# Query blocks loaded two ahead, projection weights rounded at set row blocks, scan outputs begun later

## The chip, the core and the metric

The kernel runs on one core of a Trainium2 chip. The time is the device time of one execution in microseconds (us); lower is better. TensorE (PE) multiplies matrices, VectorE (DVE), ScalarE (ACT) and GpSimd (POOL) do elementwise work, and SyncE (SP) issues nearly all transfers (DMA) of this kernel. Operands lie in SBUF, sums of products in the banks of PSUM.

## The reference

One decoder layer, float32, one sequence of 1024 tokens of width 1024. A normalised input is projected for two groups of heads that work side by side; their outputs are joined, projected and added to the input, and a squared-ReLU MLP follows. Cut to what matters:

```python
h = rms_norm(x, norm1_w)
proj = h @ w_in
da_q, da_k, da_v, dn_qkv, dn_z, dn_a, dn_b = jnp.split(proj, [...], axis=-1)
# group A: 4 heads, two 64-wide softmax maps each, causal, 128-wide values
da_q, da_k = rms_norm(da_q, q_norm_w), rms_norm(da_k, k_norm_w)
da_o = (softmax(q1 k1^T) - lam * softmax(q2 k2^T)) @ v       # per head
da_o = rms_norm(da_o, da_out_norm_w) * (1 - lam_init)
# group B: 4 heads, causal convolution, then the gated delta rule, a scan over chunks
dn_o = gated_delta_rule(dn_q, dn_k, dn_v, g, beta)
dn_o = rms_norm(dn_o, dn_out_norm_w) * silu(dn_z)
x = x + concatenate([da_o, dn_o]) @ w_out
h = rms_norm(x, norm2_w)
x = x + square(relu(h @ w_up)) @ w_down
```

## The kernel before

Products of weights and activations are made in three passes: each operand is split into a rounded part (`hH`, `wH`, type float32r) and the remainder (`hL`, `wL`), and `wH*hH + wL*hH + wH*hL` is accumulated in PSUM. A weight is therefore loaded raw (`wraw`), copied with rounding by ACT (L199) and subtracted by DVE (L200).

Up to about 239 us the gates and the projections of group B run. Then several streams are interleaved on PE by hand. Class `Interleave` (L39) holds Python generators with priorities and a planned time `now`; each `yield` says from when, or from which PSUM bank on, a stream may go on, `flow.pe` advances the time by a piece of PE work, `flow.chain` books time on the planned queues of ACT ("S"), DVE ("V") and POOL ("G") and returns when a chain of operations would be done, and `flow.hold` keeps a bank until then. The result is a fixed order of PE's instructions (L1456). The order on the other engines, SP with its transfers among them, is chosen by the framework's scheduler, which simulates a timeline; on each engine instructions then run in that order, and each waits for its operands. `tc.issue_after(ins)` keeps an instruction behind another one on the same engine.

The streams that matter here:

- `scan` (L801) and `scan_out` (L855): the delta rule over eight chunks of 128 tokens. For each chunk, `scan_out` loads two blocks per head (`pkb`, five buffers) and the gate (`zgt`), waits until 2500 ns after its start by the plan, makes two groups of products in bank `pB`, normalises and stores them. After the last chunk it sets `state["scan"]`, which lets other streams start.
- `da_units` (L940): the projections of group A in six units, (keys, queries, values) for each of two pairs of heads. A unit has 256 columns of weights in four quarters and goes over eight row blocks `tb` of 128 tokens, 24 matmuls each (L962 to L964). At block 0 of a unit, `load_unit` (L185) is called for the next unit (after the last unit, for a half of the output weights): four loads on SP's queue into two raw buffers, four roundings. Four weight buffers (`wH0`, `wH1`, `wL0`, `wL1`) alternate. `unit_time` books ACT and DVE for it and gives the planned time of each quarter. A block ends with a copy out of PSUM into `qn` (four buffers, L973 or L981); keys and queries are normalised, transposed in `da_turns` (L919) and stored to DRAM; values are stored as they are.
- `scores` (L1032): for each of 32 pairs of a head and a row block, queries are fetched by `load_q` (L1019) into `qa` and `qb` (two buffers each, four transfers), scores are made for two maps (L1082 to L1085), DVE takes the maximum (L1087), ACT the exponential (L1091). The load for the next pair is written right behind a pair's work.
- `values` (L1107): transposes the weights of a pair (L1123), copies them (L1125), multiplies by the values (L1135) into a bank of `px`, copies the result out (L1144), squares the copy for the norm (L1145) and scales it (L1149).
- `mixed` and `outproj` (L1182, L1212): transposes of the joined rows and the output projection, which fill PE beside the later attention.

From about 650 us on, the two products of the MLP run in a form with seven products in place of eight.

Of the kernel before, what the change touches and what calls it, by code (L numbers as in the profile page):

```python
# [9 lines left out]
F32 = mybir.dt.float32  # L10
# [8 lines left out]
P = 128  # L19
# [101 lines left out]
def tile_hymba_layer(  # L121
# [60 lines left out]
    hH = hpool.tile([P, KB, SEQ], F32R, name="hH")  # L182
    hL = hpool.tile([P, KB, SEQ], F32R, name="hL")

    def load_unit(src, ranges, k0=0, nk=KB, eng=None, rp=None):  # L185
        eng = eng or V
        width = sum(n for _, n in ranges)
        wh, wl = staged("wH"), staged("wL")
        wh = wh[:, :nk * width].rearrange("p (k c) -> p k c", k=nk)
        wl = wl[:, :nk * width].rearrange("p (k c) -> p k c", k=nk)  # L190
        st = 2 * UC // width
        for k in range(0, nk, st):
            raw = rp.tile([P, 2 * UC], F32, tag="wraw", name="wraw", bufs=8) if rp else laid("wraw")
            raw = raw[:, :st * width].rearrange("p (k c) -> p k c", k=st)
            o = 0
            for c0, n in ranges:
                nc.sync.dma_start(raw[:, :, o:o + n], src[:, k0 + k:k0 + k + st, c0:c0 + n])
                o += n
            S.copy(wh[:, k:k + st, :], raw)  # L199
            eng.tensor_tensor(wl[:, k:k + st, :], raw, wh[:, k:k + st, :].bitcast(F32), ALU.subtract)  # L200
        return wh, wl

    def mm3(ps, lh, ll, rh, rl, n):
# [651 lines left out]
    def scan_out(c, Sold, yy):  # L855
        pkb = {}
        for h in range(HEADS):
            pkb[h] = sb.tile([P, 2, P], F32, tag="pkb", name="pkb", bufs=5)
            nc.sync.dma_start(pkb[h], park_d[h, c, :, 3:5, :])
        zgt = sb.tile([P, 512], F32, tag="zgt", name="zgt", bufs=1)  # L860
        nc.sync.dma_start(zgt, zg_d[c])
        oc = sb.tile([P, 512], F32, tag="oc", name="oc", bufs=2)
        so = sb.tile([P, 4], F32, tag="so", name="so", bufs=2)
        osq = sb.tile([P, P], F32, tag="osq", name="osq", bufs=1)
        yield flow.now + 2500, "pB"
        if c > 0:
            o1 = pB.tile([P, 512], F32, tag="pB", name="ps_o1")
            for h in range(HEADS):
                T.matmul(o1[:, h * P:(h + 1) * P], pkb[h][:, 0, :], Sold[h], start=True, stop=True)
            V.tensor_tensor(v4(oc), v4(o1), bc_col(eg[:, c::8]), ALU.mult)  # L870
            flow.pe(4 * MM)
            flow.hold("pB", flow.chain(vec(512)))
            yield flow.now, "pB"
        o2 = pB.tile([P, 512], F32, tag="pB", name="ps_o2")
        for h in range(HEADS):
            T.matmul(o2[:, h * P:(h + 1) * P], pkb[h][:, 1, :], yy[h], start=True, stop=True)
        if c > 0:
            V.tensor_tensor(oc, oc, o2, ALU.add)
        else:
            S.copy(oc, o2)  # L880
        for h in range(HEADS):
            i = cidx(h, c)
            S.activation(osq, oc[:, h * P:(h + 1) * P], AF.Square, scale=rq[:, i:i + 1], accum_out=so[:, h:h + 1])
        f = sb.tile([P, 4], F32, tag="of", name="of", bufs=2)
        rstd(f, so, 1.0 / P, EPS, sb, "oft", 4)
        V.tensor_tensor(f, f, rq[:, c::8], ALU.mult)
        for h in range(HEADS):
            V.scalar_tensor_tensor(oc[:, h * P:(h + 1) * P], oc[:, h * P:(h + 1) * P], f[:, h:h + 1],
                                   zgt[:, h * P:(h + 1) * P], ALU.mult, ALU.mult)
        nc.sync.dma_start(mixn_d[c], oc)  # L890
        flow.pe(4 * MM)
        t = flow.chain(vec(512))
        flow.hold("pB", t)
        flow.chain(*[act(P, True)] * 4, vec(4), powr(4), vec(4), *[vec(P, 60)] * 4, start=t)
        if c == NT - 1:
            s2ctx.close()
            spctx.close()
            mp = ctx.enter_context(tc.tile_pool(name="mp", bufs=1, **left))
            pools["mp"] = mp
            for tb in tiles:  # L900
                accs[tb] = row_tile("acc")
            pools["a2"] = bctx.enter_context(tc.tile_pool(name="a2", bufs=1, **left))
            pools["be"] = bctx.enter_context(tc.tile_pool(name="be", bufs=2, **left))
            pools["rsc"] = scctx.enter_context(tc.tile_pool(name="rsc", bufs=1, space=PSUM, **right))
            state["scan"] = True
# [34 lines left out]
    def da_units():  # L940
        todo = [(g, kind) for g in range(2) for kind in (1, 0, 2)]

        def unit_w(i):
            g, kind = todo[i]
            return load_unit(w_in_v, [(512 * kind + 256 * g, 256)]), unit_time()

        w = unit_w(0)
        freed = [0.0, 0.0]
# [1 line left out]
        for i, (g, kind) in enumerate(todo):  # L950
            (wh, wl), wt = w
            for tb in range(NT):
                if tb == 0:
                    if i + 1 < len(todo):
                        w = unit_w(i + 1)
                    else:
                        pre.append((load_unit(w_out_v, [(0, 512)], 4, 4), unit_time()))
                sl = slice(tb * P, (tb + 1) * P)
                yield max(freed[n % 2], wt[0] if tb == 0 else 0.0), None
                ps = pj.tile([P, 512], F32, tag="pj", name="ps_qk")  # L960
# [7 lines left out]
                            yield wt[k // 2 + 1], None  # L968
                while len(late) > 2:
                    yield flow.now + 50, None  # L970
                qn = sd.tile([P, 256], F32, tag="qn", name="qn", bufs=4)
                if kind == 2:
                    S.copy(qn, ps[:, :256])  # L973
                    st = nc.sync.dma_start(v_d[g, tb], qn.rearrange("p (h e) -> p h e", h=2))
                    if g == 1:
                        prefetch_x(st)
                    freed[n % 2] = flow.chain(act(256))
                else:
                    sq = sd.tile([P, 256], F32, tag="qsq", name="qsq", bufs=1)
                    S.activation(sq, ps[:, :256], AF.Square)  # L980
                    S.copy(qn, ps[:, :256])  # L981
                    sn = sd.tile([P, 4], F32, tag="sn", name="sn", bufs=2)
                    V.tensor_reduce(sn, sq.rearrange("p (a d) -> p a d", d=DQK), axis=AX.X, op=ALU.add)
                    rn = sd.tile([P, 4], F32, tag="rn", name="rn", bufs=2)
                    rstd(rn, sn, 1.0 / DQK, EPS, sd, "rnt", 4)
                    qv = qn.rearrange("p (a d) -> p a d", d=DQK)
                    V.tensor_tensor(qv, qv, rn.unsqueeze(2).broadcast_to([P, 4, DQK]), ALU.mult)
                    t = flow.chain(act(256))
                    freed[n % 2] = flow.chain(act(256), start=t - flow.HOP)
                    t = flow.chain(vec(256), vec(4), powr(4), vec(256), start=t - flow.HOP)  # L990
                    late.append((g, kind, tb, qn, t))
                n += 1
                state["units"] = n
            if kind == 2:
# [22 lines left out]
        return vt  # L1017

    def load_q(h, tb):  # L1019
        qa = ap.tile([P, 2, P], F32R, tag="qa", name="qa", bufs=2)  # L1020
        qb = ap.tile([P, 2, P], F32R, tag="qb", name="qb", bufs=2)
        for s in range(2):
            src = qk_d[h // 2, 0, tb, :, s, h % 2, :].rearrange("(m p) t -> p m t", m=2)
            nc.sync.dma_start(qa[HF[s]].bitcast(F32), src)
# [7 lines left out]
    def scores():  # L1032
# [1 line left out]
        while state["da"] < 1:  # L1034
            yield flow.now + 300, None
        heads[0] = load_head(0, ap), load_v(0, ap)
        q = load_q(*order[0])
        yield state["da_t"] + 3000, None
        for u, (h, tb) in enumerate(order):
            if h == 1 and h not in heads:  # L1040
# [4 lines left out]
            if h == 2 and h not in heads:  # L1045
# [2 lines left out]
                ks = load_head(2, ap), load_head(3, pools["a2"])  # L1048
                while state["da"] < 2:
                    yield flow.now + 300, None  # L1050
                q = load_q(h, tb)
                heads[2] = ks[0], load_v(2, ap)
                heads[3] = ks[1], load_v(3, pools["a2"])
                yield state["da_t"] + 2000, None
            if q is None:
                q = load_q(h, tb)
                yield flow.now + 3000, None
            while u < 2 * NT and u > 2 + 0.4 * (state["units"] - 3 * NT) and not state["proj"]:

                yield flow.now + 100, None  # L1060
            while len(ready) > (AHEAD if state["scan"] else 0):
                yield flow.now + 100, None
            KS, vt = heads[h]
            qa, qb = q
            n = (tb + 1) * P
            npc = 1 if n <= 512 else 2
            pl = n // npc
# [32 lines left out]
            V.scalar_tensor_tensor(cf, ssum[:, 0:1], nlam, ri[:, 1:2], ALU.mult, ALU.mult)  # L1100
            V.scalar_tensor_tensor(pe[0][:, :n], pe[1][:, :n], cf, pe[0][:, :n], ALU.mult, ALU.add)
            t = flow.chain(vec(10), vec(1, 60), vec(n, 100), start=t - flow.HOP)
            if u + 1 < len(order) and order[u + 1][0] // 2 < state["da"]:
                q = load_q(*order[u + 1])
            ready.append((h, tb, pe[0], ri, vt, t))

    def values():  # L1107
        for _ in order:
# [30 lines left out]
            else:  # L1139

                om = rows_of[tb][:, h * P:(h + 1) * P]
            sq = ap.tile([P, P], F32, tag="osq2", name="osq2", bufs=1)
            so = ap.tile([P, 1], F32, tag="so2", name="so2", bufs=2)
            S.copy(om, po[:, :P])  # L1144
            S.activation(sq, om, AF.Square, scale=ri[:, 0:1], accum_out=so)  # L1145
            f = ap.tile([P, 1], F32, tag="of2", name="of2", bufs=2)
            rstd(f, so, 1.0 / P, EPS, ap, "oft2", 1)
            V.tensor_tensor(f, f, ri[:, 0:1], ALU.mult)
# [1 line left out]
            if h < 2:  # L1150
                nc.sync.dma_start(mixa_d[tb, :, h * P:(h + 1) * P], om)
            flow.pe((tb + 1) * MM)
            t = flow.chain(act(P))
            flow.hold(r, t)
            t = flow.chain(act(P, True), vec(1), powr(1), vec(1), vec(P, 60), start=t)
            if h == 3:
                loads.append((rows_of.pop(tb), t, tb, 0))
        state["attn"] = True
# [624 lines left out]
```

## Time and profile before

| | |
|---|---|
| Time, median of 3 runs | 1256.71 us (1256.1 to 1256.93) |
| Time of the profiled execution | 1258.48 us |
| Its span, first to last instruction | 1256.8 us |
| Mean granted clock of TensorE | 0.996 |

All views show one profiled execution. PE is the matmul row of TensorE and PEld its loading of weights. A name such as `qa L931` is the tile written and the line of the kernel. In the view of waits, a row tells for which instruction an engine stood idle, what ended that idle time, its total, the number of times and the longest. In the timeline, a row has start, duration, engine, line, operation, output and inputs, and in brackets the idle time before it with what ended it; equal neighbours are merged (x2). SPq and ACTq are the sequencers that issue transfers. PEclk is the clock that TensorE was granted, as a share of full speed.

### The profile page before, as it was taken

The numbers are of one execution on the slowest core, as the hardware profiler recorded it, in microseconds if no ns is written. First come the engines' busy times: TensorE is split into PE (matmuls) and PEld (weight loads), VectorE is DVE, ScalarE is ACT, GpSimd is POOL, SyncE is SP. The second block draws the span as 40 slices with busy tenths as digits, with TensorE's granted clock in tenths as the row PEclk, the third lists the DMA queues.
The fourth block names the chain that finished last, engine by engine and source line by source line (L and its number), as shares of the span: only waits on it lengthen the run. The fifth ranks groups of instructions, "written<-read, shape, count | busy, mean of one in ns | idle before, by whom it ended". The sixth has DMA issues, their size and how long they took to land.

```text
span 1256.8 us, 18942 instructions
## 1 busy us (share of the span) xinstructions
PE 1233.7 (98%) x6965; PEld 1062.8 (85%) x6965; DVE 818.1 (65%) x1416; ACT 614.5 (49%) x1239; POOL 110.8 (9%) x141
## 2 busy tenths in 40 slices
PE   9999999999998999999999999999999999999998
PEld 8978888899998997887888888888888888888887
DVE  6567797557647547776599656665568855777553
ACT  5378554334446545655566445444554333333331
POOL 3311110022212310001210000000000000000000
PEclk9999999999999999999999999999999999999999
DMA  7134554267848657322255545443469655422301
GB/s 245 43 102 128 156 158 122 74 197 240 269 139 230 174 158 190 102 68 84 85 185 168 201 151 184 151 158 129 172 228 360 244 200 201 167 101 101 131 37 67
DMA packets 163510, 197.93 MB, mean 157 GB/s; under 512 B 20649, under 2 KB 124889, under 8 KB 163418
## 3 DMA queue, kind: packets, MB, share of 16 engines
q1 hardware_dynamic: 163416, 196.72, 48.5%
q8 instruction: 55, 0.90, 0.3%
q14 instruction: 37, 0.30, 0.1%
q10 hardware_dynamic: 2, 0.00, 0.0%
HBM read 131.66 MB, written 65.01 MB: 156 GB/s over the span
## 4 chain that ended last, share of the span: by engine, by line
PE 93%; DMA 3%; ACT 1%; DVE 1%; SPq 1%; issue 1%; DVEq 0%; POOL 0%; ACTq 0%; POOLq 0%
PE X L1400 5%; PE X L1399 5%; PE X L1398 5%; PE X L1696 4%; PE X L1697 4%; PE X L1698 4%; PE ps_dn L205 3%; PE ps_dn L207 3%; PE ps_dn L206 3%; PE ps_qk L962 3%; PE ps_qk L964 3%; PE ps_qk L963 3%; PE Y L1400 2%; PE Y L1399 2%; PE Y L1398 2%; PE ps_op L1227 2%
## 5 line engine op out<-in xcount | busy, mean ns | idle before, releaser
L1316 ACT CAST hH<-ur 128x1024 fp32r<-128x1024 f32 x56 | 58.9, 1051 | 173.2 <-PE Y L1697 89.8
L1317 DVE TENSOR_TENSOR hL<-ur,hH 128x1024 fp32r<-128x1024 f32 x56 | 68.3, 1223 | 79.5 <-ACT hH L1316 79.4
L962 PE MATMUL ps_qk<-wH,hH 128*128 128x256 f32 x384 | 115.6, 301 | 0.1
L963 PE MATMUL ps_qk<-wL,hH 128*128 128x256 f32 x384 | 109.1, 284 | 0.0
L964 PE MATMUL ps_qk<-wH,hL 128*128 128x256 f32 x384 | 109.1, 284 | 0.0
L1317 DVE TENSOR_TENSOR op<-raw,op 128x1024 fp32r<-128x1024 f32 x48 | 58.7, 1223 | 75.1 <-PE X L1399 42.1
L1696 PE MATMUL X<-hH 128*128 128x512 f32 x224 | 87.1, 389 | 0.0
L1697 PE MATMUL X<-hL,hH 128*128 128x512 f32 x224 | 87.1, 389 | 0.0
L1698 PE MATMUL X<-hH,hL 128*128 128x512 f32 x224 | 87.1, 389 | 0.0
L205 PE MATMUL ps_dn<-hH,wH 128*128 128x512 f32 x192 | 76.9, 400 | 0.2 <-ACT cp L582 0.2
L207 PE MATMUL ps_dn<-hH,wL 128*128 128x512 f32 x192 | 76.5, 398 | 0.0
L206 PE MATMUL ps_dn<-hL,wH 128*128 128x512 f32 x192 | 76.2, 397 | 0.0
L962 PEld LDWEIGHTS ps_qk<-wH,hH 128*128 128x128 f32 x384 | 74.2, 193 | 0.3 <-ACT qn L981 0.2
L963 PEld LDWEIGHTS ps_qk<-wL,hH 128*128 128x128 f32 x384 | 74.2, 193 | 0.0
L964 PEld LDWEIGHTS ps_qk<-wH,hL 128*128 128x128 f32 x384 | 73.9, 192 | 0.0
L1317 DVE TENSOR_TENSOR hL<-dw,hH 128x1024 fp32r<-128x1024 f32 x56 | 68.1, 1218 | 0.8 <-ACT hH L1316 0.7
L1316 ACT CAST op<-raw 128x1024 fp32r<-128x1024 f32 x48 | 50.4, 1052 | 34.8 <-PE Y L1400 19.9
L1316 ACT CAST hH<-dw 128x1024 fp32r<-128x1024 f32 x56 | 58.7, 1048 | 10.5 <-DMA dw<-in_w_down_dram 4.9
L200 DVE TENSOR_TENSOR wL<-wraw,wH 128x512 fp32r<-128x512 f32 x64 | 43.7, 696 | 29.8 <-ACT wH L199 29.2
L586 DVE SCALAR_TENSOR_TENSOR cy<-cp,pv,cy 128x512 f32<-128x512 f32 x72 | 53.6, 745 | 14.0 <-ACT cy L584 13.3
L199 ACT CAST wH<-wraw 128x512 fp32r<-128x512 f32 x64 | 38.2, 620 | 45.2 <-DMA wraw<-in_w_in_dram 31.2
L1087 DVE TENSOR_REDUCE mx<-ps_sc 128x1 f32<-128x128 f32 (+7 forms) x64 | 47.6, 754 | 15.2 <-PE ps_sc L1085 14.7
(366 smaller groups left out, 3451.7 us busy)
## 6 DMA issues: line engine op xcount, KB each, us to landing
ur<-ud SPq DMA_DIRECT2D x28, 1024.0 KB, 5.0
raw<-in_w_up_dram SPq DMA_DIRECT2D x32, 512.0 KB, 4.4
dw<-in_w_down_dram SPq DMA_DIRECT2D x32, 512.0 KB, 6.9
wraw<-in_w_in_dram SPq DMA_DIRECT2D x48, 256.0 KB, 3.2
qk_d<-qa SPq DMA_DIRECT2D x32, 256.0 KB, 3.0
ud<-ua SPq DMA_DIRECT2D x16, 512.0 KB, 3.3
ud<-s SPq DMA_DIRECT2D x16, 512.0 KB, 2.6
pka<-park_d SPq DMA_DIRECT2D x32, 192.0 KB, 3.6
```

The costliest lines, as they stand in the source:

```text
L205: T.matmul(ps, lh(k), rh(k), start=(k == 0), stop=False)
L206: T.matmul(ps, lh(k), rl(k), start=False, stop=False)
L207: T.matmul(ps, ll(k), rh(k), start=False, stop=(k == n - 1))
L962: T.matmul(ps[:, :256], hH[:, k, sl], wh[:, k, :], start=(k == 0), stop=False)
L963: T.matmul(ps[:, :256], hH[:, k, sl], wl[:, k, :], start=False, stop=False)
L964: T.matmul(ps[:, :256], hL[:, k, sl], wh[:, k, :], start=False, stop=(k == KB - 1))
L1316: S.copy(dst[0], src)
L1317: V.tensor_tensor(dst[1], src, dst[0].bitcast(F32), ALU.subtract)
L1398: T.matmul(ps, op[0][:, k, cs], h[0][:, k, :], start=start and k == 0, stop=False, skip_group_check=True)
L1696: T.matmul(bank[t], v[0][:, j, sl], v[2][:, j], start=s0, stop=False, skip_group_check=True)
L1697: T.matmul(bank[t], v[0][:, j, sl], v[3][:, j], start=False, stop=False, skip_group_check=True)
L1698: T.matmul(bank[t], v[1][:, j, sl], v[2][:, j], start=False, stop=s1, skip_group_check=True)
```

## The change

- `load_unit` gets a parameter `later`. With it, the first two quarters are loaded at once, from ACT's queue; roundings and the loads of the other two quarters (from SP's queue) are put in a list of steps. `da_units` uses it for every unit after the first and for the first half of the output weights. After row block 1 of a unit it takes four steps (round a quarter, load the third, round the second, load the fourth), after row block 4 two steps (round the third and the fourth); each rounding is kept behind the PSUM copy of that block on ACT. In the plan the weights count as ready, and two roundings are booked at each of these blocks.
- `qa` and `qb` of `load_q` get three buffers, and `scores` keeps up to two loaded blocks ahead (`more_q`).
- `scan_out` waits 4500 ns instead of 2500 ns by the plan; `pkb` has four buffers instead of five, `qn` three instead of four.
- In `values`, the squares go into the PSUM bank itself instead of a tile of their own, and the plan holds the bank until they are made.

```diff
-    def load_unit(src, ranges, k0=0, nk=KB, eng=None, rp=None):
+    def load_unit(src, ranges, k0=0, nk=KB, eng=None, rp=None, later=None):
...
-        for k in range(0, nk, st):
+        def load(k, queue=nc.sync):
             raw = rp.tile([P, 2 * UC], F32, tag="wraw", name="wraw", bufs=8) if rp else laid("wraw")
...
-                nc.sync.dma_start(raw[:, :, o:o + n], src[:, k0 + k:k0 + k + st, c0:c0 + n])
+                queue.dma_start(raw[:, :, o:o + n], src[:, k0 + k:k0 + k + st, c0:c0 + n])
                 o += n
-            S.copy(wh[:, k:k + st, :], raw)
+            raws.append(raw)
+
+        def round_part(k, behind=None):
+            raw = raws.pop(0)
+            with tc.issue_after(behind.ins) if behind else ExitStack():
+                S.copy(wh[:, k:k + st, :], raw)
             eng.tensor_tensor(wl[:, k:k + st, :], raw, wh[:, k:k + st, :].bitcast(F32), ALU.subtract)
+
+        raws, ks = [], list(range(0, nk, st))
+        if later is None:
+            for k in ks:
+                load(k)
+                round_part(k)
+            return wh, wl
+        for k in ks[:2]:
+            load(k, nc.scalar)
+        for i, k in enumerate(ks):
+            later.append(lambda behind, k=k: round_part(k, behind))
+            if i < 2:
+                later.append(lambda behind, k=ks[i + 2]: load(k))
         return wh, wl
...
-            pkb[h] = sb.tile([P, 2, P], F32, tag="pkb", name="pkb", bufs=5)
+            pkb[h] = sb.tile([P, 2, P], F32, tag="pkb", name="pkb", bufs=4)
...
-        yield flow.now + 2500, "pB"
+        yield flow.now + 4500, "pB"
...
+        steps = []
+
         def unit_w(i):
             g, kind = todo[i]
-            return load_unit(w_in_v, [(512 * kind + 256 * g, 256)]), unit_time()
+            if i == 0:
+                return load_unit(w_in_v, [(512 * kind + 256 * g, 256)]), unit_time()
+            return load_unit(w_in_v, [(512 * kind + 256 * g, 256)], later=steps), [0.0] * 4
...
-                        pre.append((load_unit(w_out_v, [(0, 512)], 4, 4), unit_time()))
+                        pre.append((load_unit(w_out_v, [(0, 512)], 4, 4, later=steps), [0.0] * 4))
...
-                qn = sd.tile([P, 256], F32, tag="qn", name="qn", bufs=4)
+                qn = sd.tile([P, 256], F32, tag="qn", name="qn", bufs=3)
                 if kind == 2:
-                    S.copy(qn, ps[:, :256])
+                    act_at = S.copy(qn, ps[:, :256])
...
-                    S.copy(qn, ps[:, :256])
+                    act_at = S.copy(qn, ps[:, :256])
...
+                if tb in (1, 4):
+
+                    for _ in range(4 if tb == 1 else 2):
+                        steps.pop(0)(act_at)
+                    for _ in range(2):
+                        flow.chain(("S", 520.0), ("V", 610.0))
...
-        qa = ap.tile([P, 2, P], F32R, tag="qa", name="qa", bufs=2)
-        qb = ap.tile([P, 2, P], F32R, tag="qb", name="qb", bufs=2)
+        qa = ap.tile([P, 2, P], F32R, tag="qa", name="qa", bufs=3)
+        qb = ap.tile([P, 2, P], F32R, tag="qb", name="qb", bufs=3)
...
-        q = load_q(*order[0])
+        ahead_q, todo_q = [], list(order)
+
+        def more_q():
+
+            while len(ahead_q) < 2 and todo_q and todo_q[0][0] // 2 < state["da"]:
+                ahead_q.append(load_q(*todo_q.pop(0)))
+
+        more_q()
...
-                q = load_q(h, tb)
+                more_q()
...
-            if q is None:
-                q = load_q(h, tb)
-                yield flow.now + 3000, None
...
-            qa, qb = q
+            qa, qb = ahead_q.pop(0)
...
-            if u + 1 < len(order) and order[u + 1][0] // 2 < state["da"]:
-                q = load_q(*order[u + 1])
+            more_q()
...
-            sq = ap.tile([P, P], F32, tag="osq2", name="osq2", bufs=1)
...
-            S.activation(sq, om, AF.Square, scale=ri[:, 0:1], accum_out=so)
+            S.activation(po[:, :P], om, AF.Square, scale=ri[:, 0:1], accum_out=so)
...
-            t = flow.chain(act(P))
+            t = flow.chain(act(P), act(P, True))
             flow.hold(r, t)
-            t = flow.chain(act(P, True), vec(1), powr(1), vec(1), vec(P, 60), start=t)
+            t = flow.chain(vec(1), powr(1), vec(1), vec(P, 60), start=t)
```

## The prediction, made before the change was run

> **What bounds the kernel now.** I read the page's first part and then a table of five stretches.
>
> ```profile
> span 1256.8 us, 18942 instructions
> PE 1233.7 (98%) x6965; PEld 1062.8 (85%) x6965; DVE 818.1 (65%) x1416; ACT 614.5 (49%) x1239; POOL 110.8 (9%) x141
> ```
>
> ```profile
> core 0: us, PE busy (x) PEld busy (x) DVE busy (x) ACT busy (x) POOL busy (x), PEclk, DMA share, GB/s
> 238.60:469.90 231.30, 222.28 (x1897) 215.97 (x1896) 133.70 (x378) 108.18 (x320) 49.11 (x51) 0.99 0.66 197
> 469.90:600.00 130.10, 125.18 (x770) 105.17 (x769) 92.85 (x206) 77.57 (x208) 11.02 (x20) 0.99 0.40 108
> 600.00:1250.00 650.00, 649.33 (x2899) 538.07 (x2898) 420.99 (x428) 295.75 (x340) 10.75 (x13) 1.00 0.46 164
> 406.20:409.60 3.40, 3.40 (x18) 3.40 (x17) 2.77 (x7) 1.27 (x4) 0.32 (x1) 0.50 0.58 164
> 587.10:590.50 3.40, 3.40 (x10) 2.62 (x9) 1.85 (x6) 1.48 (x4) 0.00 (x0) 0.50 0.20 67
> ```
>
> TensorE is the bound, and the change takes no matmul from it. So all that can be won is time in which PE stands still, or runs at a reduced clock. The first window holds the attention projections, which the scan and the first attention heads interleave. There PE is idle 231.30 - 222.28 = 9.0 us. The next one, attention beside the output projection, has 4.9 us, and from 600 on there is 0.7 us. The edits act between 238.6 and 600, on 13.9 us of idle time. The last two rows are stretches of 3.4 us at clock 0.50: PE is busy all through and does half the work, so each costs about 1.7 us which no column of idle time shows. The third view says what PE waited for between 238 and 660:
>
> ```profile
> PE ps_qkt L927 <- ACT at L1125: 3.3, 1, 3.3
> PE ps_h L721 <- DVE W L725: 1.8, 1, 1.8
> PE ps_sc L1082 <- ACT pexp L1091: 1.7, 1, 1.7
> PE ps_at L1123 <- DVE hL L244: 1.5, 1, 1.5
> PE ps_at L1123 <- ACT mx L1144: 1.3, 1, 1.3
> PE ps_sc L1083 <- DMA qb<-qk_d: 1.1, 2, 0.9
> PE ps_sc L1082 <- DMA qa<-qk_d: 0.9, 1, 0.9
> PE ps_qkt L927 <- DVE qn L987: 0.9, 1, 0.9
> PE ps_qkt L927 <- ACT om L1144: 0.7, 1, 0.7
> ```
>
> These are a few single stalls (columns: total, times, longest). Each has to be followed back to what was really late.
>
> **The rounding of the weights** (L199 on ACT, L200 on DVE). Before, a unit's four quarters are loaded and rounded as soon as the scheduler finds room, and the second pair of loads waits for the two raw buffers. The timeline at the largest stall:
>
> ```profile
> 401.19 0.55 SPq L197 DMA_DIRECT2D wraw<-in_w_in_dram  x1
> 404.37 0.62 ACT L199 CAST wH<-wraw 128x512 fp32r<-128x512 f32 x1 [3.83 <-DMA wraw<-in_w_in_dram]
> 404.89 0.26 ACT L1125 COPY at<-ps_at 128x128 f32<-128x128 f32 x1
> 405.20 0.33 PE L927 MATMUL ps_qkt<-ident,qn 128*128 128x128 f32 x1 [3.35 <-ACT at L1125]
> ```
>
> The load goes out at 401.19. ACT has the rounding next in its order and stands 3.83 us for it. Behind it is the copy L1125 that empties a PSUM bank, and PE, which wants that bank, stands 3.35 us. The clock row from 406.2 on follows directly. After the change this quarter is loaded a whole unit ahead and rounded only behind a copy that itself waits for PE, so the wait should go: 3.35 + 1.7 = 5.05 us.
>
> ```profile
> 370.25 0.62 ACT L199 CAST wH<-wraw 128x512 fp32r<-128x512 f32 x1 [2.08 <-DMA wraw<-in_w_in_dram]
> 370.89 1.28 ACT L1091 ACT_TABLE_LOAD   x1
> 372.19 0.37 ACT L1091 ACTIVATE pexp<-ps_sc,mx 128x128 f32<-128x128 f32 x1
> 372.70 0.38 PE L1082 MATMUL ps_sc<-KS,qa 128*128 128x256 f32 x1 [1.74 <-ACT pexp L1091]
> ```
>
> The same at 370, but here the exponential's table, 1.28 us, is loaded behind the rounding and stays. Without the rounding's 0.62 us PE comes at least 0.62 us sooner; at most the whole 1.74 us goes. I take the middle, 1.2 us.
>
> ```profile
> 296.24 1.30 ACT L199 CAST wH<-wraw 128x512 fp32r<-128x512 f32 x2 [3.49 <-DMA wraw<-in_w_in_dram]
> 298.18 0.42 DVE L987 TENSOR_TENSOR qn<-qn,rn 128x256 f32<-128x256 f32 x1
> 298.75 0.30 PE L927 MATMUL ps_qkt<-ident,qn 128*128 128x128 f32 x1 [0.91 <-DVE qn L987]
> ```
>
> Here ACT stands 3.49 us, DVE's remainder L200 comes behind it, and behind that the scaling L987 for which PE waits: 0.91 us. The rounding's part is 5.05 + 1.2 + 0.91 = 7.2 us.
>
> The price of the new order. Two of the four loads of each later unit and of the first half of the output weights, 12 in all, now go out from ACT's queue. Those two waits and ACT's only issue of a load before:
>
> ```profile
> ACT wH L199 <- DMA wraw<-in_w_in_dram: 14.4, 8, 3.8
> ```
>
> ```profile
> L275 ACTq DMA_DIRECT2D hF<-in_norm_w_dram x1: 511/511/511, 0.8 to 0.8; - x1
> ```
>
> 12 x 0.511 = 6.1 us of ACT's time, against the 14.4 us that it now spends standing for these loads and the 231.30 - 108.18 = 123 us that it is idle in the window. Bounds 0 and 6.1 us on PE; I take 0.5, near the lower end, since ACT gets back more than twice what it pays. If that cover fails, PSUM copies such as L1125 are late next. The raw buffers that these loads need were released by the rounding four row blocks earlier, so nothing queues behind a wait there.
>
> The Trainium skill, "DMA: Bandwidth & Descriptors", section "Issuing engines are not separate DMA queues", says that loads issued by another engine share the same 16 DMA engines and save only the sequencer's issue time. With DMA at 0.66 of its time in the window, it speaks against any gain from the second queue as such; the sum above takes none from it.
>
> **Query blocks two ahead.** Four loads bring a block, and with two buffers the next one can start only when the block before the current one has been used.
>
> ```profile
> SPq L1024 <- PE ps_sc L1085: 24.7, 18, 5.1
> ```
>
> ```profile
> 581.76 1.37 SPq L1024 DMA_DIRECT2D qa<-qk_d  x1
> 583.84 0.58 SPq L1025 DMA_DIRECT2D qb<-qk_d  x1
> 585.13 0.30 PE L1082 MATMUL ps_sc<-KS,qa 128*128 128x128 f32 x1 [0.94 <-DMA qa<-qk_d]
> 586.31 0.30 PE L1083 MATMUL ps_sc<-KS,qb 128*128 128x128 f32 x1 [0.88 <-DMA qb<-qk_d]
> ```
>
> At the end of attention the blocks are short and follow each other in 2 to 3 us. The last one's loads are still being issued at 583.84, and PE stands 0.94 + 0.88 us, after which the clock is at 0.50 from 587.1. With a third tile these loads can start one block earlier, which is more than the 0.9 us that they lack. Gain 0.94 + 0.88 + 1.7 = 3.5 us, and the other wait of the L1083 row, 1.1 - 0.9 = 0.2 us: 3.7 us. The number of loads is unchanged. They stay on SP, whose waits (24.7 us above) begin earlier but are no longer what PE needs next.
>
> The Trainium skill, "TensorE: Matmul & The Clock Gate", asks for no PE gaps above some 3 us, and by that rule two gaps below 1 us cost no clock. The row at 587.1 shows 0.50 after them, so the measurement decides. By the rule alone the gain here would be 1.7 us smaller.
>
> **Square into PSUM, tighter buffers, later scan outputs.** L1145 now writes its squares into the bank it would otherwise have left, so the bank stays taken longer.
>
> ```profile
> L1145 ACT ACTIVATE osq<-om,ri x16: 391/402/422, 380.9 to 517.7; 128x128 f32<-128x128 f32 x16
> L1145 ACT ACTIVATION_READ_ACCUMULATOR osq<-om,ri x16: 185/187/209, 381.2 to 518.0; 128x1 f32 x16
> ```
>
> That is 0.40 + 0.19 = 0.59 us in each of 32 blocks, 18.9 us of bank time at worst. PE waits for that release (behind L1144) twice today, 1.3 and 0.7 us. I take those two places, 2 x 0.59 = 1.2 us: the rows show the other 30 releases are not awaited. A square that writes PSUM rather than SBUF has no row here; its own duration I leave as it is, with 0.1 us per block either way.
>
> qn with three tiles instead of four and pkb with four instead of five make copies and loads wait for an older reader:
>
> ```profile
> SPq L859 <- PE ps_o L876: 6.5, 7, 2.7
> ```
>
> Already today the pkb loads wait 6.5 us in seven places for the output products, and no matmul waits for pkb. Starting the outputs 2 us later moves the use by as much as the loads. Bounds: a loss of 2.7 us (one such wait passed on whole) or a gain of a few tenths; I take 0, since PE has other row blocks to run meanwhile.
>
> The planner's order of PE changes from unit 1 on, as weights count as ready and roundings are booked at fixed blocks. Of the stalls above, ps_h, ps_at and the L1144 ones are not addressed (1.8 + 1.5 + 1.3 + 0.7 = 5.3 us), and each may grow, vanish or be joined by another. Bounds: a gain of 2 us, or a new stall of the largest kind, 5.05 us. I take a loss of one of the middle size, 1.5 us.
>
> **Sum.** Gains 7.2 + 3.7 = 10.9 us, losses 0.5 + 1.2 + 0 + 1.5 = 3.2 us, net 7.7 us: a span of 1249.1. The profiled execution took 1258.48 in all, 1.7 us around its span, and the median of three runs is 1256.71, so the net is taken from the median: **1249.0 us**.
>
> **Rivals.** *The late load only moves* (the change does not do for the weights what it says). The second pair still goes through SP, behind its waits, and ACT meets it as late as before. Then only the query gain is left: 3.7 - 3.2 = 0.5 us, 1256.2. For it: SP's longest wait above is 5.1 us. Against it: the window holds 48 row blocks, 231.3 / 48 = 4.8 us each, so between the roundings at blocks 1 and 4 lie 14 us.
>
> *Slower: ACT blocked at block 4.* Roundings now have fixed places. If SP stands 5.1 us for a query buffer and again for a store, and the landing takes as long as the 401.19 load (3.2 us to 404.37), then with a rounding of 0.62 us 5.1 + 5.1 + 3.2 + 0.6 = 14 us are gone too. Then ACT blocks with PE's row block behind it, and each such unit costs what the stall at 401 did, 5.05 us. Six roundings of this kind exist (five units and the output weights). Two give 10.1 + 3.2 - 10.9 = +2.4 us, within what can be told from no change; from the third on it is slower, 1256.7 + 7.5 = 1264.2. For it: today too ACT waited at eight such places. Against it: these waits come from loads issued within 4 us of their use.
>
> *The query wait is hidden elsewhere*: the last short blocks wait for something else in the same place (softmax or a PSUM bank), and the clock still falls. Then 3.7 us are missing: 1252.7.
>
> **How the numbers follow.** Forecast 0.55, query gain lost 0.10, late load moved 0.14, blocked at block 4 0.21. This kernel can be told from no change beyond about 0.2%, 2.5 us, so faster means below 1254.2: 0.65; same 0.14; slower 0.21. The forecast's own range goes from all gains with no loss and 2 us from the new order (1256.7 - 12.9 = 1243.8) to the gains less half of the issue's 6.1, the 1.2 and half of a new stall's 5.05 (3.05 + 1.2 + 2.5 = 6.8 us: 1252.6). Reaching over the moved load and two blocked units gives 1243.5 to 1260.
>
> **What would show it.** In the new profile: ACT's wait for wraw under 5 us; no PE wait behind L1125 of 3 us and no stretch at clock 0.50 between 300 and 600; no ps_sc wait for qa or qb; PE idle in the first window near 5 us; waits behind L1145 in place of L1144. The forecast is wrong if ACT still stands 2 to 4 us before roundings, if PE's waits of the two windows still add up to 12 us or more with other names, or if a stretch at 0.50 stands elsewhere.

## The result, and the profile after

The change made the kernel slower: 1260.21 us median (22 runs) against 1257.81 us for the kernel before, measured in turn on the same chips, a ratio of 1.0025 with a 95% interval of 1.0014 to 1.0036. A second measurement gave 1.0018 (1.0003 to 1.0034). The forecast was 1249.0 us, from 1243.5 to 1260. The page and the windows of the changed kernel's profiled execution (1258.82 us):

```profile
span 1257.1 us, 18931 instructions
PE 1234.8 (98%) x6965; PEld 1062.4 (85%) x6965; DVE 822.3 (65%) x1416; ACT 616.5 (49%) x1239; POOL 109.2 (9%) x141
```

```profile
core 0: us, PE busy (x) PEld busy (x) DVE busy (x) ACT busy (x) POOL busy (x), PEclk, DMA share, GB/s
238.60:469.90 231.30, 224.30 (x1896) 216.80 (x1895) 134.84 (x378) 109.15 (x322) 47.66 (x51) 0.99 0.67 198
469.90:600.00 130.10, 124.05 (x767) 104.14 (x766) 93.99 (x203) 76.08 (x202) 10.73 (x19) 1.00 0.37 104
600.00:1250.00 650.00, 648.40 (x2896) 536.90 (x2895) 422.98 (x430) 297.44 (x345) 11.07 (x14) 1.00 0.46 164
382.30:389.10 6.80, 5.92 (x25) 4.58 (x24) 3.70 (x10) 3.76 (x11) 1.51 (x2) 0.50 0.42 127
```

In the first window PE's idle time fell from 9.0 to 7.0 us; in the second it rose from 4.9 to 6.05 and in the third from 0.7 to 1.6 us. The sum is 14.6 us both times. The two stretches at clock 0.50 around 406 and 587 are gone, and one of twice the length stands at 382. The upper rows of the view of what PE waited for between 238 and 650 are:

```profile
PE ps_o L1168 <- ACT at L1158: 3.0, 2, 2.2
PE ps_at L1156 <- ACT ps_o L1177: 2.9, 2, 2.2
PE ps_A L837 <- DVE S L866: 1.9, 1, 1.9
PE ps_at L1156 <- DVE hL L264: 1.5, 1, 1.5
PE ps_tr L258 <- DVE hL L264: 1.0, 1, 1.0
PE ps_tr L258 <- ACT ps_o L1177: 0.9, 1, 0.9
PE ps_sc L1117 <- DMA qb<-qk_d: 0.9, 1, 0.9
PE ps_h L741 <- DVE W L745: 0.7, 1, 0.7
PE ps_tr L258 <- POOL hn L1288: 0.6, 1, 0.6
PE ps_qkt L947 <- ACT ps_o L1177: 0.4, 1, 0.4
```

Every stall that the prediction meant to cure is gone. In their place stand others of the same sum, among them a query wait of 0.9 us at 383, the start of attention, where the kernel before had none. The larger of the two waits of ps_o, 2.17 of the 3.0 us (line numbers are those of the changed kernel: L951 was L931, L1158 was L1125, L1168 was L1135, L1176 and L1177 were L1144 and L1145), comes from this piece of the timeline:

```profile
376.73 0.49 SPq L953 DMA_DIRECT2D qk_d<-qa  x1
379.93 0.47 ACT L951 ACTIVATE qa<-ps_qkt,pv 128x256 fp32r<-128x256 f32 x1 [2.62 <-DMA qk_d<-qa]
380.86 0.37 ACT L1158 COPY at<-ps_at 128x256 f32<-128x256 f32 x1
381.29 0.49 PE L1168 MATMUL ps_o<-vt,at 128*128 128x128 f32 x2 [2.17 <-ACT at L1158]
```

ACT no longer stands for a weight. It now stands 2.62 us for a free buffer of the transposed queries and keys (a tile of `da_turns` that is also called `qa`), whose store was issued at 376.73. The copy that PE needs is again behind the standing instruction. The other large row, 2.9 us behind the square L1177, reads like this:

```profile
521.91 0.25 ACT L1176 COPY om<-ps_o 128x128 f32<-128x128 f32 x1
522.13 0.62 ACT L206 CAST wH<-wraw 128x512 fp32r<-128x512 f32 x1
522.66 0.58 ACT L1158 COPY at<-ps_at 128x512 f32<-128x512 f32 x1
523.13 0.38 ACT L1177 ACTIVATE ps_o<-om,ri 128x128 f32<-128x128 f32 x1
523.44 0.19 ACT L1177 ACTIVATION_READ_ACCUMULATOR ps_o<-om,ri 128x1 f32 x1
523.68 0.44 PE L1156 MATMUL ps_at<-ident,pexp 128*128 128x128 f32 x2 [2.17 <-ACT ps_o L1177]
```

The copy out of the bank ends at 522.16. The square that now keeps the bank comes only behind a rounding and another copy, and PE starts at 523.68: the bank is held 1.5 us longer, not 0.59.

### The profile page after: what moved, and what is told of

Same layout as the page of the kernel before. It is cut to its first block, busy times and chain, and to the rows that moved or that the text cites. A ratio compares the mean times of both kernels' runs of the same rounds, so it can differ in the third digit from the quotient of the medians.

```text
span 1257.1 us, 18931 instructions
## 1 busy us (share of the span) xinstructions
PE 1234.8 (98%) x6965; PEld 1062.4 (85%) x6965; DVE 822.3 (65%) x1416; ACT 616.5 (49%) x1239; POOL 109.2 (9%) x141
## 4 chain that ended last, share of the span: by engine, by line
PE 92%; DMA 3%; ACT 2%; DVE 1%; issue 1%; POOL 0%; SPq 0%; DVEq 0%; ACTq 0%; POOLq 0%
PE X L1432 5%; PE X L1430 5%; PE X L1431 5%; PE X L1729 4%; PE X L1728 4%; PE X L1730 4%; PE ps_dn L225 3%; PE ps_dn L227 3%; PE ps_dn L226 3%; PE ps_qk L986 3%; PE ps_qk L988 3%; PE ps_qk L987 3%; PE Y L1432 2%; PE Y L1430 2%; PE Y L1431 2%; PE ps_op L1259 2%
## 5 line engine op out<-in xcount | busy, mean ns | idle before, releaser
L1125 ACT ACTIVATE pexp<-ps_sc,mx 128x128 f32<-128x128 f32 (+7 forms) x64 | 47.3, 741 | 23.7 <-DVE mx L1121 23.4
L1259 PE MATMUL ps_op<-wH,hH 128*128 128x512 f32 x128 | 54.6, 426 | 0.0
```

## Experiments

All ratios are to the kernel before, measured in turn with it, with 95% intervals. A difference of two ratios carries the intervals of both, together about 0.002 to 0.003, so prices below that rest on such a difference hold to some 3 us. Theories A to F are those of the expected texts. "Behind the projections" means the time from the end of the last projection matmul to the end of the span, less 1.7 us for a 3.4 us stretch at clock 0.50 in it. It takes the clock's chance out of single profiles.

### Parts alone and parts left out

**weights_alone**: the new `load_unit` and `da_units` in the kernel before, `qn` with four tiles.

```diff
...
-            return load_unit(w_in_v, [(512 * kind + 256 * g, 256)]), unit_time()
...
+            return load_unit(w_in_v, [(512 * kind + 256 * g, 256)], later=steps), [0.0] * 4
...
```

> The kernel before with the weights' part alone (two quarters from ACT's queue, roundings behind blocks 1 and 4; query tiles, buffers, scan outputs and square as before). Theory A, the cure works and other parts give it back (bank held for the square, stores of qa awaited): ACT's waits for wraw in 238 to 470 fall from 14.4 us to under 2, PE's idle time from 238.6 to 600 falls from 13.9 us to 10 or less, and the time is 3 us or more below before. Theory B, any change of the plan draws a new set of stalls of about the same sum: ACT's waits fall just as much, but PE's idle time stays at 12 to 16 us and the time within 2.5 us of before.

Measured: 1.0026 (1.0010 to 1.0043). ACT's waits for wraw vanished, as both theories said, but the rows of PE now begin so:

```profile
PE ps_sc L1112 <- DMA qa<-qk_d: 5.8, 2, 5.2
PE ps_o L889 <- DMA pkb<-park_d: 3.0, 2, 2.9
```

```profile
372.44 0.58 SPq L1054 DMA_DIRECT2D qa<-qk_d  x1
376.42 0.58 SPq L1054 DMA_DIRECT2D qa<-qk_d  x1
380.97 0.66 PE L1112 MATMUL ps_sc<-KS,qa 128*128 128x384 f32 x1 [5.16 <-DMA qa<-qk_d]
```

PE, no longer held up by roundings, is ready for the third block of scores at 375.81, before its queries. Their two loads into `qa` go out at 372.44 and 376.42, with other transfers between them on SP's queue, and PE starts at 380.97. In the kernel before, the same loads went out at 369.32 and 370.60, and PE came to the block at 378.28 without a wait. Theory A's gain did not come: PE's idle time from 238.6 to 600 is 13.9 us as before, since the cure met a stall that had been hidden. Most of the loss stands in the clock: over the runs its mean was 0.9947, against 0.9967 of the kernel before beside it, which is 2.5 us.

**all_but_weights**: the changed kernel with `load_unit` and `da_units` of before (and `qn` with three tiles).

```diff
...
-            return load_unit(w_in_v, [(512 * kind + 256 * g, 256)], later=steps), [0.0] * 4
+            return load_unit(w_in_v, [(512 * kind + 256 * g, 256)]), unit_time()
...
```

> The changed kernel with the weights loaded and rounded as before. Theory A: ACT's waits for wraw come back (10 us or more) and with them a PE stall of 2 us or more behind a rounding; slower than the changed kernel by 3 us or more (1263). Theory B: within 2.5 us of the changed kernel (1258 to 1263), PE idle from 238.6 to 600 12 to 16 us.

Measured: 1.0048 (1.0027 to 1.0068); ACT's waits for wraw are 11.5 us again. That is 0.0023 to 0.0030 above the changed kernel: beside the other parts, the weights' part is worth some 3 to 4 us. The intervals overlap.

**all_but_queries**: the changed kernel with two query tiles and one block ahead.

```diff
-        qa = ap.tile([P, 2, P], F32R, tag="qa", name="qa", bufs=3)
+        qa = ap.tile([P, 2, P], F32R, tag="qa", name="qa", bufs=2)
...
-            qa, qb = ahead_q.pop(0)
+            qa, qb = q
```

> The changed kernel with two query tiles and one block ahead. Theory A: a ps_sc wait for qa or qb of about 1.8 us comes back near the end of attention, and the time is 2 to 4 us above the changed kernel. Theory B: within 2.5 us of the changed kernel, other stalls in its place.

Measured: 1.0063 (1.0038 to 1.0087), some 5 us above the changed kernel, with a wait for qa of 5.2 us from 373 to 378, at the start of attention as in weights_alone and not at its end, where theory A expected it. The queries' part repairs what the weights' part uncovers.

**null_scan_start**, a null run: only the plan's start of the scan is moved, and no instruction is added or removed.

```diff
-SCAN_START = 18000.0
+SCAN_START = 18400.0
```

> The kernel before with the planned start of the scan at 18.4 us instead of 18.0 us: no instruction is added or removed, only PE's planned order shifts. Theory A: within 1 us of before, the same large stalls behind roundings and query loads. Theory B: other stalls of the same sum; the time may differ by 2 us or more either way, as much as the parts of the change do.

Measured: 1.0023 (1.0005 to 1.0040). It costs about what the change does, though its profile shows the large stalls of before (3.2 and 1.7 us behind roundings). A redrawn plan alone can move the time by this much.

**before_again**, **after_again**: both kernels once more.

> The kernel before once more, unchanged, for a second profile on this chip. If stalls are fixed by the order of the instructions (theory A's ground), the same rows come back within 0.5 us each and PE's idle time from 238.6 to 640 is 14 to 15 us; if they also hang on when transfers land, some of them differ by 1 us or more and the stretches at clock 0.50 stand elsewhere.

> The changed kernel once more on the same chip as before_again. Theory B: ratio 1.001 to 1.004, waits of ACT at qa for the store qk_d again 5 us or more, PE idle from 238 to 640 14 to 16 us. Theory A, with the new waits only a matter of one execution: under 12 us, ratio 1.000 or less.

Measured: 1.0001 (0.9985 to 1.0017) and 1.0018. The waits come back: before_again has 3.4, 1.9, 1.6, 1.5, 1.5 us in its first rows, after_again 3.3, 2.9, 1.6, 1.5, 1.0. So the stalls belong to the order of the instructions and to no single execution, and ACT's 8.8 us of waits for the store in after_again too. The clock does not come back:

```profile
78.50:81.90 3.40, 3.40 (x17) 2.81 (x16) 1.61 (x4) 3.37 (x9) 0.00 (x0) 1.00 0.61 154
402.70:406.10 3.40, 2.83 (x13) 2.83 (x14) 2.79 (x6) 2.95 (x8) 0.00 (x0) 0.50 0.52 155
587.10:590.50 3.40, 3.40 (x26) 2.83 (x25) 2.56 (x10) 2.65 (x11) 0.55 (x1) 1.00 0.57 157
```

Of before's stretches at 78, 406 and 587 only the one at the 3.4 us stall is there again. The waits for the query loads at the end, 0.8 and 1.0 us, stood in before_again as well and cost no clock; in the profiles of null_scan_start and weights_alone the stretch at 587 is there.

**no_store_wait**: all_but_queries with a third tile for the store that ACT waits for.

```diff
-            qa = sd.tile([P, 2, 256], F32R, tag="qa", name="qa", bufs=2)
+            qa = sd.tile([P, 2, 256], F32R, tag="qa", name="qa", bufs=3)
```

> As all_but_queries, with three tiles instead of two for the transposed queries and keys that wait for their store (qa of L949). If ACT's wait for that store is what costs (theory D), it goes and the time falls by 2 us or more below all_but_queries (ratio 1.0063 to 1.0045 or less). If not, the ratio stays at 1.005 or more, with the query stall of 5 us still there.

Measured: 1.0053 (1.0037 to 1.0070), 0.001 lower, within the intervals. The wait for the store is gone from ACT, but the query stall (4.8 us) is not, and the time hardly moves. Theory D is not borne out by this kernel, in which ACT waited only 3.3 us for that store. The changed kernel, where ACT waits 9.0 us for it, was not tried with a third tile, so for it theory D stays open.

### The bank

**square_alone**: the square's two edits on the kernel before.

```diff
-            S.activation(sq, om, AF.Square, scale=ri[:, 0:1], accum_out=so)
+            S.activation(po[:, :P], om, AF.Square, scale=ri[:, 0:1], accum_out=so)
...
-            t = flow.chain(act(P))
+            t = flow.chain(act(P), act(P, True))
             flow.hold(r, t)
-            t = flow.chain(act(P, True), vec(1), powr(1), vec(1), vec(P, 60), start=t)
+            t = flow.chain(vec(1), powr(1), vec(1), vec(P, 60), start=t)
```

> The kernel before with the squares written into the PSUM bank and the bank held for them in the plan; nothing else. If the longer hold is what the second stage loses (theory C: all three kernels with it had 7.4 to 8.1 us of idle time from the last projection to the last output product, the three without 5.2 to 5.6), that idle time is 7 us or more with waits behind the square, and the time 2 us or more above before. If it is the redrawn plan alone (theory B), the idle time is anywhere from 5 to 8 us and the waits behind the square stay below 2 us.

Measured: 1.0015 (1.0000 to 1.0030). From the last projection to the last output product PE is idle 8.4 us (5.6 before), with 6.5 us of waits behind the square in three rows. These are the signs of theory C, but the order of PE is another one too. The next two runs separate the two.

**square_psum_old_plan** has the first of these two edits, and PE's order is the one of before; **square_sbuf_new_plan** has the second, and PE's order is the one of square_alone.

> The kernel before with the squares in the PSUM bank, but the plan's hold as before, so that PE's order is the one of before, instruction by instruction. If the bank's real hold costs (theory C in hardware): waits of ps_at, ps_tr and ps_qkt behind the square grow by 0.6 us at each of some four places, ratio 1.001 to 1.003, 787 us or more behind the last projection. If only the plan's booking costs: ratio 0.999 to 1.001, about 785 us.

> The kernel before with the squares in SBUF as before and only the plan's hold of the bank lengthened to the square's end: PE's order changes, no instruction is longer. If the plan's booking costs: about 787.5 us behind the last projection and ratio 1.001 to 1.003, as square_alone. If the real hold costs: about 785 us and ratio 0.999 to 1.001.

Measured: 1.0031 (1.0017 to 1.0045) and 0.9958 (0.9944 to 0.9972). In equal orders of PE the bank's real hold costs 0.0031 on the old plan, and 1.0015 - 0.9958 = 0.0057 on the new one: 4 to 7 us. The traces show PE's 6965 instructions in the same order in each pair; on ACT, DVE and SP some tens stand at other places. Waits of the first of the two:

```profile
PE ps_at L1123 <- ACT ps_o L1145: 3.2, 5, 1.5
PE ps_qkt L927 <- ACT ps_o L1145: 2.8, 4, 1.1
```

```profile
381.17 0.26 ACT L1144 COPY om<-ps_o 128x128 f32<-128x128 f32 x1
381.31 0.59 ACT L1091 ACTIVATE pexp<-ps_sc,mx 128x384 f32<-128x384 f32 x1
381.88 0.38 ACT L1145 ACTIVATE ps_o<-om,ri 128x128 f32<-128x128 f32 x1
382.17 0.20 ACT L1145 ACTIVATION_READ_ACCUMULATOR ps_o<-om,ri 128x1 f32 x1
382.43 0.33 PE L927 MATMUL ps_qkt<-ident,qn 128*128 128x128 f32 x1 [1.01 <-ACT ps_o L1145]
```

Nine waits, 6.0 us, where before had two, 2.0 us, at two of the same releases; the other seven banks were free before PE came. An exponential runs between copy and square, so the hold grows by 0.94 us here. The booking alone, with a bank that is free early, was worth 0.42%, outside both expected ranges. That is the fastest kernel of the study, 1249.24 us. Of its gain some 2.5 us stand in the clock (mean 0.9989 over the runs, against 0.9969 of the kernel before beside it). Why its order is better is not shown: the plan keeping PE away from the bank may do it, or one redrawn order may simply be luckier than another.

**after_order_square_in_at**: the changed kernel, squares written into `at`; PE's order stays that of the changed kernel. **after_square_in_at** has the old booking besides.

```diff
-            S.activation(po[:, :P], om, AF.Square, scale=ri[:, 0:1], accum_out=so)
+            S.activation(ats[-1][:, :P], om, AF.Square, scale=ri[:, 0:1], accum_out=so)
```

> The changed kernel with only the destination of the squares moved from the PSUM bank to the copied weights (tile at); the plan stays, so PE's order is that of the changed kernel. If the bank's real hold is what made the change slow (theory C): the waits behind the square (4.2 us in both profiles) fall by 2.5 us or more, the ratio is 0.995 to 0.998, 4 to 7 us below the changed kernel. If not: 1.000 to 1.003.

> The changed kernel with the squares written into the copied weights (tile at, whose last reader is done by then) instead of the PSUM bank, and the plan's hold of the bank as before. Theory C (the bank's longer hold costs what the other parts gain): the time from the last projection's end on falls by 2 to 3 us (from 787.5 to about 785 us, without stretches at clock 0.50), and the ratio to before is 0.997 to 1.000. Theory B (any new plan costs about as much): ratio 1.001 to 1.004 and 787 us or more.

Measured: 0.9981 (0.9961 to 1.0001) and 0.9974 (0.9959 to 0.9989). The same order on PE without the bank's hold is 0.0037 to 0.0044 faster than the changed kernel, about 5 us (PE's order is equal in the traces too). The waits of the first:

```profile
PE ps_o L1168 <- ACT at L1158: 3.0, 2, 2.2
PE ps_sc L1117 <- DMA qb<-qk_d: 1.5, 1, 1.5
PE ps_at L1156 <- DVE hL L264: 1.5, 1, 1.5
PE ps_A L837 <- DVE S L866: 1.2, 1, 1.2
PE ps_at L1156 <- ACT om L1176: 1.0, 1, 1.0
PE ps_tr L258 <- DVE hL L264: 1.0, 1, 1.0
```

Of 4.2 us behind the square, 1.0 us behind the copy is left; the 3.0 us of ps_o stay. Behind the projections all seven profiles with the squares in the bank have 787.5 to 789.1 us, the thirteen without them 783.6 to 785.6 us.

### What the rest is worth with the bank free

**after_loads_on_SP**: after_square_in_at with all loads on SP's queue.

```diff
-            load(k, nc.scalar)
+            load(k)
```

> after_square_in_at with the first two quarters of each unit loaded from SP's queue instead of ACT's. If ACT's issue time is a cost (at most 12 x 0.5 us): ratio lower than after_square_in_at by 0.001 or more. If SP's queue is what delays stores and query loads: higher by 0.001 or more, with longer waits of ACT for the store qk_d. Else within 0.001.

Measured: 0.9981 (0.9966 to 0.9995) against 0.9974: no difference. The second queue neither costs nor brings anything that can be seen. By the Trainium skill, "DMA: Bandwidth & Descriptors", section "Issuing engines are not separate DMA queues", a second issuing engine saves only issue time, and this agrees.

**all_but_weights_square_in_at**: after_order_square_in_at with the weights' functions of before. **weights_new_plan**: weights_alone on square_sbuf_new_plan.

> As after_order_square_in_at, with the weights loaded and rounded as in the kernel before. If the weights' part is worth something once the bank is free: ratio above after_order_square_in_at by 0.002 or more, ACT's waits for wraw 10 us or more with a PE stall behind a rounding. If roundings only move stalls about: within 0.0015 of it.

> The weights' part alone on square_sbuf_new_plan (0.9958). If it gains as forecast where the bank is free: 0.993 or less. If one query block ahead is too little beside it (as in weights_alone, with a stall of 5.2 us for qa): 0.997 or more, with a ps_sc wait for qa of 2 us or more.

Measured: 1.0013 (0.9994 to 1.0032) and 0.9999 (0.9980 to 1.0018). With the queries two ahead the weights' part is worth 0.0032, 4 us, as it was with the bank held. With one block ahead it costs 0.0041, 5 us, with a wait for qa of 5.4 us.

**new_plan_buffers**, **new_plan_buffers_scan**: square_sbuf_new_plan with the first two of these lines, then with all three. **after_order_scan_2500**: after_order_square_in_at with the third undone.

```diff
-            pkb[h] = sb.tile([P, 2, P], F32, tag="pkb", name="pkb", bufs=5)
+            pkb[h] = sb.tile([P, 2, P], F32, tag="pkb", name="pkb", bufs=4)
...
-                qn = sd.tile([P, 256], F32, tag="qn", name="qn", bufs=4)
+                qn = sd.tile([P, 256], F32, tag="qn", name="qn", bufs=3)
...
-        yield flow.now + 2500, "pB"
+        yield flow.now + 4500, "pB"
```

> square_sbuf_new_plan (0.9958) with four pkb and three qn tiles; PE's order stays. If the tighter buffers cost (theory E): ratio 0.998 or more, with waits behind qn or pkb of 2 us or more. If they are free, as the prediction took them: 0.994 to 0.9975.

> As new_plan_buffers, with scan outputs 2 us later in the plan. If the later start costs (theory F: a new order, other stalls in the scan's chain such as ps_o behind oc, 2 us or more): 0.002 or more above new_plan_buffers. If free: within 0.0015 of it.

> after_order_square_in_at (0.9981) with scan outputs at 2500 ns again. Theory F: 0.996 or less. If the later start is needed with four pkb tiles: 0.999 or more, with a wait for pkb of 2 us or more. If neither: 0.9965 to 0.999.

Measured: 0.9965 (0.9952 to 0.9977), 1.0043 (1.0028 to 1.0058) and 0.9988 (0.9976 to 1.0000). The buffers are free within the intervals. The later start costs 0.0078 where queries come one block ahead, again through one row:

```profile
PE ps_sc L1082 <- DMA qa<-qk_d: 6.2, 1, 6.2
```

In the changed kernel's setting, two blocks ahead and with the weights' part, it is worth nothing either way (0.9988 against 0.9981; theory F is wrong there), with waits for pkb of 2.0 us when it is undone.

## Why the prediction was wrong, point by point

Two of its own signs of being wrong are there: PE's idle time in the two windows is still 13.05 us, mostly under other names, and a stretch at clock 0.50 stands elsewhere, at 382. It had given 0.21 to a slower kernel, but by ACT blocked at block 4, which did not happen.

**The square's bank was mis-sized, and that decided.** "I take those two places, 2 x 0.59 = 1.2 us: the rows show the other 30 releases are not awaited." Measured in equal orders of PE: 4 and 7 us on the kernel before, 5 us on the changed one. Two things were wrong. A release that nobody awaits has some slack, but the view of waits doesn't say how much, and it was less than the added hold in seven more places. And the hold does not grow by the square's own 0.59 us but by whatever ACT does between copy and square: 0.94 us at 381, 1.5 us at 522. With the squares elsewhere the change is a gain of 2 to 3 us (0.9981, whose interval reaches 1.0001, and 0.9974).

**The new order was mis-sized too.** "I take a loss of one of the middle size, 1.5 us." Without the bank's hold and its price of 1.2 us the forecast was a gain of 8.9 us; 2 to 3 came. In after_order_square_in_at the stalls that before didn't have (ps_o 3.0, ps_A 1.2, ps_tr 1.0 and the growth of the qb wait from 1.1 to 1.5) make 5.6 us. Other rows shrank, so that the span less PE's busy time fell by 4.3 us (1256.8 - 1233.7 to 1249.6 - 1230.8), where the forecast took 7.5 us of gain from stalls and 3.4 us from the clock. The null and the booking alone show how far a redrawn order goes without any instruction becoming longer: from 1.0023 down to 0.9958, a loss of 3 us or a gain of 5. Nothing measured stood behind the 1.5 us. How much of what is missing is the new order and how much the weights' shortfall below can't be told apart, so the two must not be added.

**The weights' mechanism was right, its size about half.** ACT's 14.4 us of waits for wraw went to nothing and no clock stretch stayed at 406. But the 7.2 us were read off as if nothing else stood behind those stalls. Left out of the changed kernel, with the bank held or free, the part is worth 3 to 4 us; alone it loses 3 us, about as much as the null, and the next thing late there is the query load at the start of attention. The rivals by which the load would be late again did not happen: ACT's waits for the later quarters are not in the list.

**The queries.** The forecast saw the wait at the end of attention (3.7 us with its clock). The part is worth about 5 us in the changed kernel, at another place: it covers the 5.2 us stall that other parts open at the start of attention (373 to 378 in all_but_queries).

**The clock.** The forecast took 2 x 1.7 us from the stretches at 406 and 587, read from one execution. before_again has the same waits and no stretch at 587, and the changed kernel's new stalls brought stretches of their own. Over the runs the mean clock was 0.9971 in after_again and 0.9968 in the kernel before beside it: 0.4 us.

**The small terms.** ACT's issues (0.5 us taken) and the buffers (0) cost nothing that can be seen. The later start was right at 0 in the changed kernel; without the queries' and the weights' parts it costs 0.0078.

**What stays open.** Stalls and clock of single profiles put the changed kernel within 1 us of the kernel before (14.6 us idle each), while the medians differ by 2.4 us. The profiled executions are not the median ones: before's, 1258.48 us, lies 0.7 us above its median and the changed kernel's, 1258.82 us, 1.4 us below its own, so the traces show too little of the difference. By the mean clocks above it is not the clock; it could not be put to one line. Nor is it shown what the null loses: between 238.6 and 600 PE is idle 13.9 us in both, and of the rows of 0.9 us and more only a ps_o wait of 1.4 us came and the qn wait went.

## What to carry to other kernels

Before an edit lengthens the hold of a buffer that rotates between streams, measure its slack, and count what the engine may run between the old last reader and the new one; writing the unwanted result into a tile that is already dead took about 5 us off here. Where a plan fixes the order of the busiest engine, try an edit of the plan alone, and a null, first: they moved the time by as much as the parts did. Parts that cure each other's stalls must be judged by leaving one out, not by adding one.

## What the runs showed of the hardware

TensorE's clock goes with much of the spread between executions of one kernel. Over 22 runs of the changed kernel the granted clock lay between 0.993 (span 1263.0 us) and 1.000 (1254.1 us). A difference of 0.007 would be 8.8 us of a span of 1257 us.

The stretches at 0.50 last 3.4 us or a multiple (6.8 us at 382), and the same stalls did or did not bring one. It goes by how a stall falls on a grid. In each of the twenty traces all stretches begin on one grid of 3.41 us. From 20 us on, every grid window in which PE was busy less than 44% was followed by a stretch, 24 of 24. Of the windows between 44 and 60% 17 of 54 were, and at full clock none above. In the kernel before both query waits at the end fall into one window, 583.69 to 587.10, with PE busy 1.59 us. In before_again they fall into two, 580.20 to 583.61 and 583.61 to 587.02, with 2.17 and 2.86 us, and no stretch follows. So a stall of 2 us may or may not cost 1.7 us of clock; as a sum it can't be added.

ACT's square took less time when it wrote to PSUM than to SBUF. In square_psum_old_plan:

```profile
L1145 ACT ACTIVATE ps_o<-mx,ri 128x128 f32<-128x128 f32 x16 | 6.0, 375 | 0.4
L1145 ACT ACTIVATE ps_o<-om,ri 128x128 f32<-128x128 f32 x16 | 6.0, 373 | 0.3
```

These are 374 ns on the mean, against 402 and 405 ns in the two rows of the kernel before. It is a gain of 0.03 us per block on an engine that does not set the end.
